# S5 input projections taken out of the preparation and placed around the latents and among the first attention heads

## The chip, the cores and the metric

The kernel runs on one core of one Trainium2 chip. The metric is the device time of one launch in microseconds (us). TensorE (PE) does the matrix products, with its weight loads listed apart as PEld; VectorE (DVE), ScalarE (ACT) and GpSimd (POOL) do elementwise work; SyncE (SP) issues every DMA transfer of this kernel, one after the other from a single queue.

## The reference, cut to what matters

Two layers over 512 tokens of width 1024. The S5 branch takes `u_b`, 1024 of the columns of one combined input projection; the MLA branch takes its latents `c_q` and `c_kv` from the same projection.

```
for l in range(DEPTH):                       # DEPTH = 2
    h = rms_norm(x, pre_norm[l])
    proj = h @ w_in[l]
    z_a, xbc, dt_raw, u_b, z_b, c_q, c_kv, k_rope, z_c, gate_logits = split_columns(proj)
    y_a = ssd_branch(...) @ w_a[l]
    y_b = s5_branch(u_b, z_b, ...) @ w_b[l]  # 64 groups of 16 channels, complex-diagonal scan
    y_c = mla_branch(c_q, c_kv, k_rope, z_c, ...) @ w_c[l]      # 16 heads
    merged = gate_0 * y_a + gate_1 * y_b + gate_2 * y_c
    x = x + rms_norm(merged @ w_o[l], post_norm[l])
```

## The kernel before, in words

Every float32 product is made of three matmuls of a high and a low part. One projection (`proj`, `dense`) takes a tile of 128 output columns: a DMA loads the weights to `wf` (512 KB), ACT rounds them to the high part `wh`, DVE (in the heads every third time POOL) makes the low part `wl`, and PE runs 24 matmuls of 128x512 (lines 116, 117 and 119) on the normed input `hh`, `hl`. `wf`, `wh` and `wl` have two buffers each.

A layer begins with the latents: four projections for `c_q`, two for `c_kv`, each group followed by `normed`. In it PE sums squares (line 225), POOL makes the inverse root `rs_r`, DVE puts it on diagonals (`tmp<-ident,rs_r`), PE spreads it over the partitions (line 231), DVE and ACT scale the latents and split them in `cqh`, `cql`, `ckh`, `ckl`. Then come 16 attention heads. Of head `h+1` the scores are made (`aux<-kh,qh`) before head `h` goes on: DVE masks them and takes the maximum (line 612, then `nm`), ACT makes the exponentials, PE transposes them (line 634), ACT and DVE split them (`ph`, `pl`), PE multiplies with the values (lines 644 to 647). Per pair of heads `make_q` and `make_k` make queries and keys; `ql<-mm,qh` is DVE's share of a query. After each odd head DVE multiplies the pair's output with its gate: `keep<-tmp,keep`, two operands in SBUF.

The S5 preparation `s5_prep` is a generator whose steps run between these parts, whenever `fill(n)` asks for n of them. Its first step makes coefficients on DVE, of which `p_fr` is late and the start of POOL's work. Then follow eight blocks of eight groups. `block` is a step of its own: a projection, a copy `pu` by ACT, a store to the DRAM tensor `ud`, eight transfers back that gather it in another order (`puf`), a store of that to `u2`, three loads of the coefficients `bc`, seven small operations. Then there are four steps `front` (six POOL operations on `pw` and `pv`) with the `back` of the step before: two PE transposes (line 368), splits, matmuls `pM`, every second time a matmul `pk` of full float32 (line 385), and in the fourth a store `msd<-pmo`. There are 42 steps, and the calls of `fill` ask for 42.

After the heads DVE scans the states (`s5_scan`, lines 891 to 894, after a load of `msd`), while PE multiplies with `w_c` and makes gates, with `ah` from the heads' output as its input; the SSD stage, the S5 output and the output projection follow.

The order of each engine's instructions, SP's included, is fixed when the program is made, by a scheduler that goes by the order of the code, by the buffers and by its own idea of durations. On an engine an instruction that waits holds all behind it.

## Time and profile before

| | |
|---|---|
| median of 3 runs | 2001.6 us (2001.11 to 2006.5) |
| the profiled execution | 1999.34 us, of which the span from first to last instruction is 1997.5 us |
| PE, PEld busy | 1883.4 us (94%), 1530.5 us (77%) |
| DVE, ACT, POOL busy | 1448.1 us (72%), 941.1 us (47%), 645.6 us (32%) |
| granted TensorE clock, mean over the span | 0.965 |

A clock of 1 is the higher of TensorE's two levels, 2.4 GHz, and 0.5 the lower, 1.2 GHz; a mean of 0.86 over a stretch says that it stood at the lower level for 28% of it. In a list by time, the number in brackets behind an instruction is the idle time of its engine before it, with what ended that time.

### The profile page before, as it was taken

What the parts mean: (1) busy time and instruction counts of PE and PEld (TensorE: products, weight loads), DVE (VectorE), ACT (ScalarE), POOL (GpSimd) and SP (SyncE); (2) the same over time, 40 slices, a digit from 0 to 9 for tenths busy, and PEclk for the clock granted to TensorE, in tenths of its full rate; (3) what the DMA queues carried; (4) which work ended last, traced back from release to release, by engine and by line L of the source; (5) the groups of instructions that cost most, each with busy time, mean ns of one, the idle gap of its engine ahead of it and who ended that gap; (6) DMA issues with size and microseconds to landing.
All of it is one profiled execution on the core that took longest, in us unless ns stands there. A gap on an engine that the chain in (4) does not pass through costs nothing.

```text
span 1997.5 us, 27806 instructions
## 1 busy us (share of the span) xinstructions
PE 1883.4 (94%) x9688; PEld 1530.5 (77%) x9688; DVE 1448.1 (72%) x2845; ACT 941.1 (47%) x1743; POOL 645.6 (32%) x743
## 2 busy tenths in 40 slices
PE   7897999899999989999998999998999999999998
PEld 5685777687887778888876777776878887788887
DVE  6866667699999857744579666677999996666443
ACT  4364556522555545543333655564235563555431
POOL 1855467301233201201118556672013331012010
PEclk9898999899999999999998999998999999899999
DMA  5333244232312266345223333342232224662541
GB/s 159 94 115 86 88 116 121 74 120 81 131 64 73 70 172 182 106 132 177 96 84 88 112 104 111 91 140 83 96 122 78 75 74 111 182 173 85 166 130 42
DMA packets 132605, 219.96 MB, mean 110 GB/s; under 512 B 36208, under 2 KB 75760, under 8 KB 131952
## 3 DMA queue, kind: packets, MB, share of 16 engines
q1 hardware_dynamic: 132464, 218.19, 36.0%
q8 instruction: 76, 1.25, 0.2%
q14 instruction: 65, 0.53, 0.1%
HBM read 182.08 MB, written 31.33 MB: 107 GB/s over the span
## 4 chain that ended last, share of the span: by engine, by line
PE 59%; DVE 24%; DMA 8%; POOL 3%; ACT 3%; issue 2%; SPq 1%; DVEq 0%; POOLq 0%; ACTq 0%
PE mm L116 13%; PE mm L117 13%; PE mm L119 12%; DVE wl L78 4%; DMA wf<-in_w_in 3%; DVE keep L69 3%; PE mm L61 2%; PE mm L62 2%; PE mm L63 2%; DVE ms L894 2%; DVE sc_t L891 2%; PE pk L385 2%; DVE ms L893 1%; PE aux L61 1%; PE aux L62 1%
## 5 line engine op out<-in xcount | busy, mean ns | idle before, releaser
L116 PE MATMUL mm<-hh,wh 128*128 128x512 f32 (+1 forms) x1232 | 500.9, 407 | 16.0 <-DVE ql L78 8.8
L117 PE MATMUL mm<-hl,wh 128*128 128x512 f32 (+1 forms) x1232 | 493.5, 401 | 0.0
L66 ACT ACTIVATE wh<-wf 128x1024 fp32r<-128x1024 f32 (+1 forms) x294 | 291.4, 994 | 422.9 <-PE mm L117 232.7
L78 DVE TENSOR_TENSOR wl<-wf,wh 128x1024 fp32r<-128x1024 f32 (+1 forms) x243 | 297.0, 1227 | 180.6 <-ACT wh L66 151.9
L119 PE MATMUL mm<-hh,wl 128*128 128x512 f32 (+1 forms) x1232 | 315.4, 393 | 3.8 <-DVE wl L78 3.8
L116 PEld LDWEIGHTS mm<-hh,wh 128*128 128x128 f32 (+1 forms) x1232 | 237.3, 193 | 77.9 <-DVE ql L78 9.9
L117 PEld LDWEIGHTS mm<-hl,wh 128*128 128x128 f32 (+1 forms) x1232 | 236.7, 192 | 50.0 <-issue 1.9
L119 PEld LDWEIGHTS mm<-hh,wl 128*128 128x128 f32 (+1 forms) x1232 | 227.7, 187 | 53.3 <-DVE wl L78 4.6
L81 POOL TENSOR_TENSOR mg<-mg,tmp 128x512 f32<-128x512 f32 x32 | 77.4, 2420 | 461.4 <-DVE tmp L78 244.0
L81 POOL TENSOR_TENSOR wl<-wf,wh 128x1024 fp32r<-128x1024 f32 (+1 forms) x51 | 109.0, 2138 | 291.2 <-PE mm L119 185.9
L116 PE MATMUL mm<-ah,wh 128*128 128x512 f32 x512 | 200.6, 394 | 0.0
L117 PE MATMUL mm<-al,wh 128*128 128x512 f32 x512 | 199.8, 391 | 0.0
L119 PE MATMUL mm<-ah,wl 128*128 128x512 f32 x512 | 127.6, 390 | 0.0
L116 PEld LDWEIGHTS mm<-ah,wh 128*128 128x128 f32 x512 | 96.5, 189 | 21.6 <-issue 1.8
L117 PEld LDWEIGHTS mm<-al,wh 128*128 128x128 f32 x512 | 96.3, 188 | 20.6 <-DVE keep L78 0.5
L119 PEld LDWEIGHTS mm<-ah,wl 128*128 128x128 f32 x512 | 95.7, 188 | 19.5
L612 DVE CUSTOM_DVE_ANT_0 sc<-aux,cmask 128x128 f32<-128x128 f32 (+3 forms) x128 | 60.3, 485 | 50.2 <-PE aux L63 48.4
L81 POOL TENSOR_TENSOR pv<-pq,ar 128x288 f32<-128x288 f32 x64 | 56.7, 906 | 86.3 <-PE pk L385 69.8
L66 ACT ACTIVATE sc<-sc,nm 128x128 f32<-128x128 f32 (+3 forms) x128 | 70.3, 553 | 28.7 <-DVE nm L73 28.7
L78 DVE TENSOR_TENSOR pl<-aux,ph 128x512 fp32r<-128x512 f32 (+1 forms) x96 | 54.7, 593 | 25.6 <-ACT ph L66 25.2
L69 DVE SCALAR_TENSOR_TENSOR keep<-mm,cw,keep 128x511 f32<-128x511 f32 (+2 forms) x96 | 71.0, 740 | 2.1 <-ACT keep L66 1.5
L66 ACT ACTIVATE tmp<-mm 128x512 f32<-128x512 f32 x76 | 44.8, 593 | 58.5 <-PE mm L63 32.3
(344 smaller groups left out, 4083.4 us busy)
## 6 DMA issues: line engine op xcount, KB each, us to landing
wf<-in_w_in SPq DMA_DIRECT2D x156, 512.0 KB
odr<-pv SPq DMA_DIRECT2D x64, 128.0 KB
wf<-in_w_c SPq DMA_DIRECT2D x16, 512.0 KB
wf<-in_w_a SPq DMA_DIRECT2D x16, 512.0 KB
wf<-kpad SPq DMA_DIRECT2D x128, 64.0 KB
wf<-odr SPq DMA_DIRECT2D x16, 512.0 KB
wf<-in_w_glu SPq DMA_DIRECT2D x16, 512.0 KB
wf<-in_w_b SPq DMA_DIRECT2D x16, 512.0 KB
```

What stands on the lines that cost most here:

```text
L61: mm(out, ah, bh, start=start, stop=False)
L62: mm(out, ah, bl, start=False, stop=False)
L63: mm(out, al, bh, start=False, stop=stop)
L66: self.nc.scalar.activation(out, in_, func, **kw)
L69: self.nc.vector.scalar_tensor_tensor(out, in0, s, in1, op0, op1)
L78: self.nc.vector.tensor_tensor(out, a, b, op)
L81: self.nc.gpsimd.tensor_tensor(out, a, b, op)
L116: mm(ps[:m], wh[:, o(i)], bh, start=i == 0, stop=False)
L117: mm(ps[:m], wh[:, o(i)], bl, start=False, stop=False)
L119: mm(ps[:m], wl[:, o(i)], bh, start=False, stop=i == k - 1)
L385: nc.tensor.matmul(pk.rearrange("p g k -> p (g k)"), bbp[b % 2][:, q:q + 4].rearrange("p g h -> p (g h)"), v1[:, :, 0:8].rearrange("p g k ...
L612: nc.vector.tensor_tensor_reduce(out=sc, in0=ps[:, :n], in1=self.cmask[:, 512 - n:512], op0=ALU.add, op1=ALU.max, scale=1.0, scalar=-3.0e3 ...
```

## The change

The projection of a block becomes a method `s5_u` of its own, called by `inputs(n)` from `mla`: two after the latents' projections, one after `normed` of `c_q`, one after `normed` of `c_kv`, and one each in heads 1, 3, 5 and 7. Its copy `pu` is stored by eight transfers (16 partitions, pieces of 64 floats) straight to `u2`, which now has the final order; the tensor `ud` and the gather are gone. In the preparation `load(b)` takes the finished block (`puf`) from `u2` and the `bc` coefficients, one block ahead: it is called in the third step of the block before. `block` is no step any more but opens the first `front`; 34 steps remain, and `fill` asks for 3 steps after every fourth head and for 2 after the others. Half of `bc` gets a second buffer, `pu`, `puf` and `pmo` one buffer each in place of two shared by all three, and a scratch size of the program is lowered.

```diff
--- before.py
+++ after.py
@@ -230,6 +230,16 @@
         pr = self.bank()
         nc.tensor.matmul(pr, self.ones, dg, start=True, stop=True)
         return pr
+
+    def s5_u(self, l, pp, b):
+
+        ps = self.proj(l, UB + b)
+        u = pp.tile([P, 512], F32, name="pu", tag="pu").rearrange("p (j c) -> p j c", j=8)
+        self.act_(u[:, ::-1], ps.rearrange("p (c j) -> p j c", j=8))
+        for g in range(8):
+            self.nc.sync.dma_start(
+                self.u2[b, :, 64 * g:64 * g + 64].rearrange("(j h) c -> h j c", j=8), u[16 * g:16 * g + 16],
+            )
 
 
     def s5_prep(self, l, pp):
@@ -292,40 +302,35 @@
         zero = pp.tile([16, 112], F32, name="zero", tag="pkf")
         nc.vector.memset(zero, 0.0)
         d = lambda nm, shape: self.dr.tile(shape, F32, name=f"{nm}{l}")
-        kpad, odr, msd, u2 = d("kpad", [16, 64, 240]), d("odr", [P, 64, P]), d("msd", [2, 64, 2, 32, 64]), d("u2", [8, P, 512])
-        ud = d("ud", [8, 8, 16, 8, 64])
+        kpad, odr, msd, u2 = d("kpad", [16, 64, 240]), d("odr", [P, 64, P]), d("msd", [2, 64, 2, 32, 64]), self.u2
         nc.sync.dma_start(kpad[:, :, 0:112], zero.unsqueeze(1).broadcast_to([16, 64, 112]))
         self.s5m[l] = (kpad, odr, msd, u2, sc1, sc2)
         yield
         NB = 2
         et = self.gt
-        pf = lambda nm: pp.tile([P, 512], F32, name=nm, tag="pf", bufs=2)
 
         bbp = [pt(f"pbb{i}", [P, 8, 32]) for i in range(2)]
         for t in bbp:
             nc.gpsimd.memset(t, 0.0)
 
-        def block(b):
-
-            ps = self.proj(l, UB + b)
-            u = pf("pu").rearrange("p (j c) -> p j c", j=8)
-            self.act_(u[:, ::-1], ps.rearrange("p (c j) -> p j c", j=8))
-            nc.sync.dma_start(ud[b].rearrange("g h j c -> (g h) j c"), u)
-            uf = pf("puf")
-            for j in range(8):
-                nc.sync.dma_start(
-                    uf[16 * j:16 * j + 16].rearrange("h (g c) -> h g c", g=8),
-                    ud[b, :, :, j].rearrange("g h c -> h g c"),
-                )
-            nc.sync.dma_start(u2[b], uf)
+        def load(b):
+
+            uf = pt("puf", [P, 512])
+            nc.sync.dma_start(uf, u2[b])
             g8 = slice(8 * b, 8 * b + 8)
-            x1, x2 = (pt(n, [P, 8, 2, 16]) for n in ("bc1", "bc2"))
+            x1, x2 = pt("bc1", [P, 8, 2, 16]), pt("bc2", [P, 8, 2, 16], 2)
             nc.sync.dma_start(x1, a["s5_bc"][l, :, g8])
             nc.sync.dma_start(x2[0:64], a["s5_bc"][l, 64:128, g8])
             nc.sync.dma_start(x2[64:128], a["s5_bc"][l, 0:64, g8])
+            return uf, x1, x2
+
+        def block(b, uf, x1, x2):
+
+            g8 = slice(8 * b, 8 * b + 8)
             b1, b2, c1, c2 = x1[:, :, 0], x2[:, :, 0], x1[:, :, 1], x2[:, :, 1]
             fb = lambda x: x[:, g8].unsqueeze(2).broadcast_to([P, 8, 16])
-            u1, bs, q1 = (pt(n, [P, 8, 16]) for n in ("pu1", "pbs", "pq1"))
+            u1 = pp.tile([P, 8, 16], F32, name="pu1", tag="pv2")
+            bs, q1 = (pt(n, [P, 8, 16]) for n in ("pbs", "pq1"))
             bb = bbp[b % 2][:, :, 0:16]
             et(bb, b1, fb(fr), ALU.mult)
             et(u1, b2, fb(fis), ALU.mult)
@@ -360,7 +365,7 @@
             if s == 0:
                 u = keep["u"] = pp.tile([P, 8, 2, 64], F32R, name="pu2", tag="pu2")
                 self.split(uf.rearrange("p (g c) -> p g c", g=8), u[:, :, 0], u[:, :, 1])
-                keep["mo"] = pf("pmo").rearrange("p (g c) -> p g c", g=8)
+                keep["mo"] = pt("pmo", [P, 512]).rearrange("p (g c) -> p g c", g=8)
                 nc.gpsimd.memset(keep["mo"][:, :, 0], 0.0)
             u, mo = keep["u"], keep["mo"]
             pm = self.pq.tile([P, 512], F32, name="pm", tag="pb")
@@ -400,15 +405,16 @@
             if s == 3:
                 nc.sync.dma_start(msd[b // 4, :, :, 8 * (b % 4):8 * (b % 4) + 8].rearrange("p r g c -> r p g c"), mo)
 
-        todo = None
+        todo, nxt = None, load(0)
         for b in range(8):
-            blk = block(b)
-            yield
+            blk = block(b, *nxt)
             for s in range(4):
                 vw = front(b, s, *blk)
                 if todo:
                     back(*todo)
                 todo = (b, s, blk[0], blk[1], *vw)
+                if s == 2 and b < 7:
+                    nxt = load(b + 1)
                 yield
         back(*todo)
 
@@ -473,7 +479,7 @@
         self.gt(mg, mg, g, ALU.add)
 
 
-    def mla(self, l, fill):
+    def mla(self, l, fill, inputs):
         nc, tc, a = self.nc, self.tc, self.a
         with tc.tile_pool(name=f"mla{l}", bufs=1, reuse_waits="tile") as mp:
             qn, kvn = mp.tile([P, 4], F32, name="qn"), mp.tile([P, 2], F32, name="kvn")
@@ -504,9 +510,12 @@
 
             fill(1)
             cq, ckv = latent(CQ, 4), latent(CKV, 2)
+            inputs(2)
             cq = normed(*cq, qn, "cq")
+            inputs(1)
             fill(1)
             ckv = normed(*ckv, kvn, "ck")
+            inputs(1)
 
             def rope(ps, n):
                 sw, r = self.tmp(), self.tmp()
@@ -590,10 +599,12 @@
                     make_k(h // 2 + 1)
                 if h % 4 == 0:
                     make_v(h // 4)
+                if h % 2 == 1 and h < 8:
+                    inputs(1)
                 if h < 15:
                     pr[h + 1] = self.attend_qk(mp, q[h + 1], kt[(h + 1) % 2], h + 1)
                 values(h)
-                fill(3 if h % 2 else 2)
+                fill(3 if h % 4 == 3 else 2)
             self.lo_pool = 0
 
     def attend_qk(self, mp, q, k, h):
@@ -982,13 +993,21 @@
         self.yc = []
         with ExitStack() as pst:
             pp = pst.enter_context(tc.tile_pool(name=f"prep{l}", bufs=1, reuse_waits="tile", side="right"))
+            self.u2 = self.dr.tile([8, P, 512], F32, name=f"u2{l}")
+            todo_u = list(range(8))
+
+            def inputs(n):
+                for b in todo_u[:n]:
+                    self.s5_u(l, pp, b)
+                del todo_u[:n]
+
             prep = self.s5_prep(l, pp)
 
             def fill(n):
                 for _ in range(n):
                     next(prep, None)
 
-            self.mla(l, fill)
+            self.mla(l, fill, inputs)
             fill(99)
         with tc.tile_pool(name=f"act{l}", bufs=8, reuse_waits="tile") as self.act:
             self.mix(l)
@@ -1214,7 +1233,7 @@
     from concourse.bass_utils import run_bass_kernel_spmd
 
     arrays = layouts(inputs)
-    nc = bacc.Bacc("TRN2", target_bir_lowering=False, num_devices=1)
+    nc = bacc.Bacc("TRN2", target_bir_lowering=False, num_devices=1, dynamic_dma_scratch_size=1024)
     aps = {
         n: nc.dram_tensor(f"in_{n}", v.shape, mybir.dt.from_np(v.dtype), kind="ExternalInput").ap()
         for n, v in arrays.items()
```

How the order of the instructions changes is shown at three places of the first layer. The first is POOL, where the latents are normed: `rs_r` is the inverse root that PE waits for, everything else down to the second row of `pbb` belongs to the preparation, except `wl` and `tmp`. Before:

```order
L81 TENSOR_TENSOR pw_1184<-pbb_757,ar 128x256
L81 TENSOR_TENSOR wl<-wf,wh 128x1024
L81 TENSOR_TENSOR pv_1324<-bc_806,ai 128x288
L81 TENSOR_TENSOR pbs<-pbs,pu_810 128x128
L81 TENSOR_TENSOR rs_r<-rs_v,mhalf 128x4
L81 TENSOR_TENSOR tmp<-tmp 128x512
L81 TENSOR_TENSOR pbb_758<-bc_1390,p_fr 128x8x16
```

Now:

```order
L81 TENSOR_TENSOR pv_1493<-bc_886,ai 128x288
L81 TENSOR_TENSOR pv_1331<-pv_1331,pv_1493 128x288
L81 TENSOR_TENSOR pu_1515<-bc_1369,p_fis 128x128
L81 TENSOR_TENSOR pbb_880<-pbb_880,pu_1515 128x8x16
L81 TENSOR_TENSOR rs_r<-rs_v,mhalf 128x4
L81 TENSOR_TENSOR pu_1515<-bc_1368,p_fi 128x128
L81 TENSOR_TENSOR wl<-wf,wh 128x1024
L81 TENSOR_TENSOR rs_r<-rs_v,mhalf 128x4
```

From `p_fr` on, 15 POOL operations (one of them a `wl`) stood ahead of the first `rs_r`; now it is 25, without a `wl`, and the inverse roots of both latents stand close together. In the second layer the count goes from 5 to 20. On PE, 48 projection matmuls (two projections) stood between line 225 and line 231 of `c_q`; now two more projections stand ahead of line 225, 31 matmuls between the two, and 41 behind them, ahead of the first `cqh`.

The second place is SP's queue in the same stretch. `u_388` is the DRAM tensor `u2`, `wf<-in_w_uq` and `wf<-in_w_ukv` are weights that the latents meet next. Now:

```order
L240 DMA u_388<-pu 16x8x64 x8
L102 DMA wf<-in_w_in 128x1024
L361 DMA odr_571<-pv_900 128x2x128
L319 DMA puf<-u_388 128x512
L361 DMA odr_571<-pv_1331 128x2x128
L240 DMA u_388<-pu 16x8x64 x8
L102 DMA wf<-in_w_uq 128x512
L361 DMA odr_571<-pv_1331 128x2x128
L319 DMA puf<-u_388 128x512
L322 DMA bc_1750<-in_s_bc 128x256
L240 DMA u_388<-pu 16x8x64 x8
L102 DMA wf<-in_w_uq 128x512
```

Four groups of eight stores now stand among these weight loads (the fourth, ahead of `wf<-in_w_ukv`, isn't shown), and two loads `puf` that must wait until the stores of the same block have landed. Before, one store `ud` and one group of eight gathers stood there, behind all three of these weight loads.

The third place is PE at the end of the heads, ahead of the first matmul with `w_c` (`mm<-ah,wh`). `pm`, `pM` and `pk` belong to the preparation. Before:

```order
L1009 MATMUL aux<-ident,rs 16x128 x4
L368 MATMUL pm<-ident,pw_4093 128x128 x2
L645 MATMUL aux<-pl,v_3574 64x256
L647 MATMUL aux<-ph,v_3574 128x256
...
L368 MATMUL pm<-ident,pw_4127 128x128 x2
L377 MATMUL pM<-pu_4041,pmh 128x128
L1021 MATMUL aux<-r_4262,sel 128x512 x3
L378 MATMUL pM<-pu_4041,pml 128x64
...
L385 MATMUL pk<-pv_4091,pbb_758 128x512
L1021 MATMUL aux<-r_4262,sel 128x512 x2
L116 MATMUL mm<-ah,wh 128x512
```

Now:

```order
L656 MATMUL aux<-pl,v_3734 64x384
L658 MATMUL aux<-ph,v_3734 128x384
L1028 MATMUL aux<-ident,rs 16x128 x4
L656 MATMUL aux<-pl,v_3734 64x256
L658 MATMUL aux<-ph,v_3734 128x256
L656 MATMUL aux<-pl,v_3734 64x128
L658 MATMUL aux<-ph,v_3734 128x128
L1040 MATMUL aux<-r_4253,sel 128x512 x5
L116 MATMUL mm<-ah,wh 128x512
```

Between the last scores and the first matmul with `w_c` PE had four pairs of `pm`, sixteen `pM` and three `pk` to do; of these one `pk` and four `pM` are left there.

## Rows read from the trace of the kernel before

**Rows 1.** Windows by stage: length, busy time (count) by engine, then clock, DMA share, GB/s.

```profile
core 0: us, PE busy (x) PEld busy (x) DVE busy (x) ACT busy (x) POOL busy (x), PEclk, DMA share, GB/s
62.40:111.70 49.30, 39.65 (x163) 30.21 (x162) 37.19 (x57) 17.40 (x34) 40.09 (x54) 0.86 0.35 100
111.70:368.20 256.50, 235.07 (x1221) 193.52 (x1220) 165.13 (x341) 147.23 (x364) 149.70 (x221) 0.93 0.36 105
368.20:398.40 30.20, 25.00 (x94) 16.90 (x92) 23.35 (x49) 16.43 (x42) 8.57 (x16) 0.72 0.23 56
...
500.00:700.00 200.00, 194.77 (x1062) 157.94 (x1063) 184.67 (x296) 109.47 (x179) 62.58 (x43) 0.99 0.25 84
1055.00:1101.50 46.50, 37.89 (x154) 28.18 (x153) 41.87 (x71) 16.63 (x32) 41.67 (x53) 0.89 0.31 87
1101.50:1353.20 251.70, 235.87 (x1229) 193.52 (x1228) 166.75 (x343) 146.58 (x365) 153.93 (x225) 0.95 0.38 110
1353.20:1385.00 31.80, 26.03 (x95) 17.22 (x93) 23.45 (x49) 16.79 (x42) 8.67 (x16) 0.73 0.23 55
```

**Rows 2.** Timeline of PE in layer 1's latents: start, length, instruction.

```profile
56.99 0.39 PE L116 MATMUL mm<-hh,wh 128*128 128x512 f32 x1
...
62.43 0.95 PE L225 MATMUL aux<-ones,tmp 128*128 128x1 f32 x8
...
77.72 1.12 PE L231 MATMUL aux<-tmp,ones 128*128 128x512 f32 x2 [3.30 <-DVE tmp L73]
...
111.71 0.97 PE L61 MATMUL aux<-kh,qh 96*128 96x128 f32 x3
```

**Rows 3.** Timeline of PE in layer 2's latents.

```profile
1055.02 0.95 PE L225 MATMUL aux<-ones,tmp 128*128 128x1 f32 x8
...
1067.89 1.13 PE L231 MATMUL aux<-tmp,ones 128*128 128x512 f32 x2 [1.56 <-DVE tmp L73]
...
1100.35 0.57 PE L61 MATMUL aux<-kh,qh 96*128 96x128 f32 x3
```

**Rows 4.** Timeline of POOL in layer 1's and layer 2's latents.

```profile
61.88 1.45 POOL L81 TENSOR_TENSOR pbb<-bc,p_fr 128x128 f32<-128x128 f32 x1 [2.19 <-DVE p_fr L78]
...
73.62 1.02 POOL L81 TENSOR_TENSOR rs_r<-rs_v,mhalf 128x4 f32<-128x4 f32 x1
...
1059.40 0.45 POOL L81 TENSOR_TENSOR pbb<-bc,p_fr 128x128 f32<-128x128 f32 x1 [1.78 <-DVE p_fr L78]
```

**Rows 5.** Timeline of SP's queue in layer 1's latents: one group of eight issues.

```profile
77.48 3.82 SPq L316 DMA_DIRECT2D puf<-ud  x8
```

**Rows 6.** The chain that ended last: two stores, start and time to landing.

```profile
175.09 7.77 DMA msd<-pmo
...
1152.76 2.00 DMA ud<-pu
```

**Rows 7.** Timelines of DVE, POOL and PE around the end of head 3.

```profile
150.74 4.87 DVE L78 TENSOR_TENSOR keep<-tmp,keep 128x512 f32<-128x512 f32 x1
...
147.19 1.36 POOL L81 TENSOR_TENSOR pv<-pq,ar 128x288 f32<-128x288 f32 x2 [0.80 <-PE pk L385]
...
155.14 0.97 POOL L81 TENSOR_TENSOR pw<-pbs,ai 128x256 f32<-128x256 f32 x1
...
156.39 0.80 PE L116 MATMUL mm<-hh,wh 128*128 128x512 f32 x1 [4.25 <-DVE ql L78]
```

**Rows 8.** Windows around the same gap, columns as in rows 1.

```profile
152.00:168.00 16.00, 11.75 (x45) 9.16 (x46) 10.67 (x14) 6.05 (x17) 5.37 (x8) 0.79 0.13 42
164.00:172.00 8.00, 8.00 (x40) 6.32 (x39) 6.76 (x10) 3.81 (x9) 5.33 (x7) 1.00 0.34 94
```

**Rows 9.** Timeline of PE in layer 2: the last gap of that kind.

```profile
1360.92 0.39 PE L645 MATMUL aux<-pl,v 128*64 128x384 f32 x1 [2.79 <-DVE pl L78]
```

**Rows 10.** Groups by form, DVE, 111.7 to 368.2: busy us, mean ns | idle before.

```profile
L78 DVE TENSOR_TENSOR keep<-tmp,keep 128x512 f32<-128x512 f32 x7 | 15.7, 2249 | 0.0
L612 DVE CUSTOM_DVE_ANT_0 sc<-aux,cmask 128x512 f32<-128x512 f32 x15 | 10.3, 685 | 1.1 <-PE aux L63 0.5
```

**Rows 11.** Waits over the span: total us, times, longest us.

```profile
POOL pu L81 <- DMA bc<-in_s_bc: 34.3, 13, 6.7
```

**Rows 12.** Timelines of PE and DVE at the end of layer 1's heads.

```profile
367.93 0.39 PE L63 MATMUL aux<-kh,ql 96*128 96x512 f32 x1
...
391.40 0.79 PE L116 MATMUL mm<-ah,wh 128*128 128x512 f32 x1
...
371.98 3.19 DVE L73 TENSOR_SCALAR nm<-mx 128x4 f32<-128x4 f32 x1
...
404.83 0.28 DVE L891 TENSOR_TENSOR sc_t<-sc,ms 128x64 f32<-128x64 f32 x1
```

## The prediction

> **What bounds the kernel now.** The page's first part gives PE 94% of the span, so PE comes first: what PE doesn't use is idle time or clock. I therefore went from the page to windows by stage, and in each stage took its length less PE's busy time, plus the share of it at the missing clock (1 less the mean clock, times the length). For layer 1's latents, 49.30 us long with 39.65 busy at 0.86, that is 9.65 + 6.9 = 16.6 us [rows 1]. In the same way layer 2's latents give 13.7, the heads 39.4 and 28.4, the ends of the heads 13.7 and 14.4. Together 126 us of 1997.5; the change touches all six stretches and cannot win more than that. The rest of the span is almost full, as 500 to 700 us shows: 194.77 of 200 busy at 0.99. DVE has 184.67 there [rows 1], so work moved toward that stretch finds little free.
>
> **The latents.** The work is only moved: one projection is 24 matmuls, 62.43 - 56.99 = 5.44 us of PE, 0.227 us each [rows 2]. What can be won is PE's wait inside this stretch. Line 231 starts at 77.72 after 3.30 us idle [rows 2], although two projections lie between it and line 225. It waits for a chain: POOL's `rs_r`, which starts at 73.62 [rows 4], then DVE's `tmp`, so 77.72 - 73.62 = 4.1 us from `rs_r` to line 231. POOL had begun at 61.88, when `p_fr` came, and did 15 operations in 11.74 us [rows 4]; one was the long `wl`, which I put at 2.4, the others at 0.67.
>
> Now POOL has 25 operations before `rs_r`, without `wl`: 25 x 0.69 = 17.3 us, so `rs_r` starts at 61.9 + 17.3 = 79.2 and line 231 can start at 83.3. PE has two projections more ahead of line 225 (62.43 + 10.9 = 73.3) and 31 matmuls behind it (7.0), and is ready at about 80.4. The wait stays, some 2.9 us. Line 231 and small steps take 2, then come 41 matmuls (9.3), 66 more up to the first scores (24 of a projection, 36 of queries, 6 of keys: 15.0) and 2.5 of small ones: first scores at 83.3 + 2 + 9.3 + 15.0 + 2.5 = 112.1, against 111.71 [rows 2]. By then three more projections (16.3 us) are done, so the best case is a gain of 16.3 - 0.4 = 15.9. The worst is first scores at 125.7: a wait of 2.8 for the first keys, two spells at half clock that lose 3.4 each (the price of one, below), 4 for late weights (SP, below), a gain of 2.3. I take 118.5, in between, since each of these has its counterpart in the trace but not all need come: gain 9.5.
>
> Layer 2 by the same steps: line 225 goes from 1055.02 [rows 3] to 1065.9; 33 matmuls more give 1073.4. POOL starts at 1059.40 [rows 4] and has 20 operations (14.0) instead of 5, so `rs_r` starts at 1073.4, line 231 at 1077.5 after 4.1 idle, where it was 1.56 [rows 3]. First scores: 1105 at best, 1118.6 at worst, I take 1111.5 against 1100.35 [rows 3], 11.2 later with 16.3 done: gain 5 (11.7 to -2). Latents together: **-14.5**.
>
> **SP's queue.** A block has ten transfers and three of `bc` now, and nine and three after: nothing is saved or lost in issues (eight take 3.82 us [rows 5]). What can be late: `puf` is behind its own eight stores and ahead of the weights for queries and keys, and SP goes in order. While `puf` waits for the stores to land, the weights are not issued. The stores write pieces of 256 bytes. Nothing before does exactly that; the nearest rows are `msd`, in pieces of 256 bytes too, 7.77 us to landing, and `ud`, in long rows, 2.00 [rows 6]. With the first, the weights come up to 4 us late at one place per layer (in the worst case above); with the second not at all. The Trainium skill speaks against the new layout: "DMA: Bandwidth & Descriptors", section "Specifications", asks for transfers of at least 512 bytes for the full rate and says that below it the engine reads, modifies and writes. The two landing times agree in direction, though other queueing may be in them. Elsewhere a late `puf` costs nothing, for it is loaded one block ahead.
>
> **The heads.** Three of the seven projections that stood in the heads are in the gain above; the four that remain stand in heads 1 to 7, none in heads 8 to 15. There PE filled with them the time in which it would have waited for masks, exponentials and splits. So some idle time opens: nothing at best, since queries, keys and preparation still fill in; at worst the present idle rate of 256.50 - 235.07 = 21.4 us [rows 1] doubles in half the heads and a bit falls on other work, some 8. I take 3 per layer: **+6**.
>
> **The end of the heads.** From the last scores (367.93) to the first matmul with `w_c` (391.40) PE needs 23.5 us [rows 12], at clock 0.72 [rows 1]: the preparation's last steps and the last head wait for each other. Most of these steps move ahead of it. What is left is the last head's own chain, about 14 us by the same timeline (mask, exponentials, transposes, products). PE's share of the moved steps, some 5 us, is paid earlier. 23.5 - 14 - 5 = 4.5, I take 4 per layer (0 if the chain keeps its length, 9 if the moved work finds free places): **-8**. DVE's `nm`, 3.19 us for 128x4 [rows 12], is in that chain and would be short with POOL quiet.
>
> **The scan.** It begins at 404.83 [rows 12], after the last `msd`, and could begin some 10 us sooner. But what follows it is held by DVE's 184.67 of 200 [rows 1], so at most part arrives: 0 to 8 per layer, I take 2: **-4**. The second `bc` buffer and the smaller scratch I cost at nothing: POOL's waits for `bc`, 34.3 us in 13 times [rows 11], are on an engine 32% busy, and PE asks for its results a step later. What their loss could do is the first rival.
>
> Sum: -14.5 + 6 - 8 - 4 = -20.5, from 1999.3 to 1979; the median lies 2.3 above the profiled execution, so I forecast **1980**. All the good ends together give 2001.6 - 27.6 - 18 - 16 = 1940, all the bad ones 2001.6 - 0.3 + 16 = 2017; they don't come together, so the forecast's own range is 1962 to 1993. What a measurement of this kernel tells from no change is about 0.3%, 6 us.
>
> **Rivals.** *Slower: POOL stands in DVE's way more often.* At the end of head 3, DVE's `keep<-tmp,keep`, two operands in SBUF, takes 4.87 us from 150.74, while POOL goes from one piece to the next from 147.19 to beyond 155.14; it ends only at 155.61. Behind it in DVE's order is `ql`, and PE stands 4.25 us for it at 156.39 [rows 7]. Then the clock falls: 0.79 over 152 to 168, 3.4 us lost, and 1.00 behind it [rows 8]. The seven `keep` of these heads have a mean of 2249 ns where `sc<-aux,cmask` of the same size, one operand not in SBUF, has 685 [rows 10]. I count seven such gaps of PE in both layers, the first [rows 7] and the last, 2.79 us [rows 9], 21.5 us together: 3.1 each and 3.4 of clock, 6.5 us. The Trainium skill names it: "GPSIMD Engine Reference", section "8. Key points", says that the engine shares its SBUF interfaces with VectorE, in contention with DVE instructions that have two SBUF inputs; the 4.87 us agree. Now POOL waits for `bc` no more, a block's small operations run into the first `front`, and nine fronts stand in four heads where there were eight: longer runs without a break. Three more hits eat the gain (3 x 6.5 = 19.5), from the fourth or fifth on it is slower than before; if all 16 ends of odd heads were hit, nine more, 1980 + 58 = 2038. Against it: the work of POOL is the same, it merely has another place, and a hit needs POOL's run and `keep` together. Four to six more, 2006 to 2019, is how it would come: 2012. Chance 0.2.
>
> *Given back.* PE has the same matmuls as before. If heads 8 to 15 open as much idle time as the latents win, the time stays at 2001, give or take 6. For it: PE is 92% busy in the heads. Against: the stretches with most loss per us are the latents and the ends, and both get filled. Chance 0.2.
>
> *SP late.* If the stores land as slowly as `msd` and the weights wait each time, the latents come near their worst ends, 2.3 - 2 = 0.3 where I take 14.5. With two thirds of that lost the time is 1980 + 10 = 1990, at the most 1994: a smaller gain. Chance 0.2.
>
> **Numbers.** Forecast 0.4, SP late 0.2, given back 0.2, slower 0.2. Faster by over 0.3% means below 1995.6: the forecast, nearly all of SP late, and a little of given back: 0.61. Within: most of given back: 0.17. Slower, above 2007.6: the first rival and a tail of the second: 0.22. For 8 in 10 the range goes from 1960 to 2014.
>
> **What would show it.** In the profile after: line 231 at about 83 with 2 to 4 us idle; first scores near 118 and 1111; POOL's wait for `bc` mostly gone; last scores to `w_c` some 14 to 18 us; new idle time in heads 8 to 15 of a few us; the number of PE gaps behind `keep` near seven. Wrong would make me: twelve or more of these gaps, weights for queries landing after PE is ready, or latents that end beyond 125.

## The result, and the profile after

The changed kernel takes 2019.63 us (median of 4 runs, 2016.97 to 2021.86), the kernel before 2001.36 beside it: ratio 1.0085, 95% interval 1.0064 to 1.0106. It is slower by 0.85%, beyond the range that was given. The profiled execution has a span of 2020.0 us, 22.5 more than before. All intervals below are of the ratio to the kernel before, timed on the same chip as the run.

The page of the changed kernel, first part, engines' busy time:

```profile
span 2020.0 us, 27725 instructions
PE 1876.6 (93%) x9688; PEld 1533.8 (76%) x9688; DVE 1429.4 (71%) x2847; ACT 938.8 (46%) x1743; POOL 633.2 (31%) x741
```

PE does the same 9688 matmuls and is busy 6.8 us less than before; the lost time is idle. Windows by stage (columns as in [rows 1]; latents, heads and ends of the heads of both layers, 500 to 700, and then heads 0 to 7 and 8 to 14 of each layer apart):

```profile
72.40:119.30 46.90, 40.55 (x169) 31.50 (x167) 26.59 (x48) 15.64 (x27) 23.72 (x27) 0.93 0.46 114
119.30:378.30 259.00, 228.50 (x1188) 188.18 (x1187) 166.52 (x348) 145.85 (x374) 162.13 (x248) 0.93 0.34 94
378.30:409.70 31.40, 17.89 (x74) 11.91 (x73) 20.67 (x63) 14.54 (x32) 0.31 (x1) 0.78 0.26 79
500.00:700.00 200.00, 193.22 (x1030) 157.21 (x1029) 181.81 (x287) 108.40 (x176) 58.86 (x40) 0.97 0.26 83
1081.90:1124.30 42.40, 39.83 (x170) 31.32 (x169) 29.79 (x50) 16.92 (x31) 28.57 (x33) 0.92 0.49 123
1124.30:1381.70 257.40, 223.99 (x1186) 184.71 (x1185) 172.74 (x347) 144.45 (x370) 160.64 (x246) 0.94 0.34 95
1381.70:1412.20 30.50, 17.25 (x72) 11.64 (x71) 20.78 (x69) 13.48 (x31) 0.31 (x1) 0.78 0.26 81
119.30:263.00 143.70, 130.35 (x664) 107.43 (x663) 84.39 (x185) 79.83 (x202) 87.38 (x129) 0.94 0.35 94
263.00:375.70 112.70, 95.55 (x506) 78.19 (x505) 80.38 (x157) 65.04 (x170) 74.75 (x120) 0.91 0.32 91
1124.30:1262.50 138.20, 125.18 (x661) 103.91 (x660) 88.94 (x184) 79.08 (x198) 85.90 (x127) 0.96 0.36 98
1262.50:1379.00 116.50, 96.11 (x505) 78.14 (x505) 81.83 (x156) 64.15 (x171) 74.69 (x120) 0.91 0.31 89
```

The same halves of the heads before:

```profile
111.70:249.70 138.00, 122.35 (x628) 101.16 (x627) 87.84 (x178) 75.77 (x187) 71.63 (x106) 0.93 0.33 96
249.70:364.70 115.00, 109.22 (x575) 89.55 (x573) 74.36 (x157) 68.96 (x170) 76.19 (x114) 0.94 0.41 120
1100.30:1235.40 135.10, 125.43 (x644) 103.36 (x644) 89.28 (x182) 76.29 (x190) 75.75 (x111) 0.94 0.36 104
1235.40:1349.70 114.30, 108.14 (x574) 88.35 (x573) 75.79 (x157) 68.86 (x170) 77.41 (x114) 0.96 0.41 120
```

"Loss" below is what the prediction used: length less PE's busy time, plus length times missing clock. The latents lose 9.6 and 6.0 us where they lost 16.6 and 13.7 [rows 1]: 14.7 won. The heads lose 48.6 and 48.8, before 39.4 and 28.4: 29.6 more. The ends lose 20.4 and 20.0, before 13.7 and 14.4: 12.3 more. In the heads the loss lies in one half: heads 8 to 14 go from 12.7 and 10.7 to 27.3 and 30.9; heads 0 to 14 together from 66.5 to 98.7, of which PE's idle time makes 37.3 and 63.9 and the clock the rest. Three projections have left heads 8 to 14 (575 matmuls before, 506 now), 16.3 us of work, and its length went from 115.0 to 112.7 and from 114.3 to 116.5. Heads 0 to 7 lose 22.0 and 18.5, before 25.3 and 17.8.

At the end of layer 1's heads, timelines of DVE, PE and SP's queue:

```profile
388.61 0.48 DVE L701 MEMSET dtraw<- 32x512 f32 x1
397.36 0.27 DVE L902 TENSOR_TENSOR sc_t<-sc,ms 128x64 f32<-128x64 f32 x1 [8.27 <-DMA ms<-msd]
397.83 0.68 DVE L69 SCALAR_TENSOR_TENSOR tmp<-aux,tmp 64x512 f32<-64x512 f32 x1
398.85 0.68 DVE L78 TENSOR_TENSOR r<-tmp,r 32x512 fp32r<-32x512 f32 x1
```

```profile
399.68 3.12 PE L1040 MATMUL aux<-r,sel 64*128 64x512 f32 x5 [9.98 <-DVE r L78]
402.73 0.79 PE L116 MATMUL mm<-ah,wh 128*128 128x512 f32 x1
```

```profile
381.25 0.56 SPq L406 DMA_DIRECT2D msd<-pmo  x1
...
389.36 0.32 SPq L898 DMA_DIRECT2D ms<-msd  x1
...
390.21 0.42 SPq L672 DMA_DIRECT2D alog<-in_a_log  x1
```

PE needs `r`. Its operands come by 391.2 (ACT's last copy), but DVE's order has the scan's first `sc_t` ahead of it, and that waits for `ms`, a load that waits on SP for the last `msd` to land (6.8 us, to 389.36). Before, the scan began at 404.83 [rows 12], behind `r`.

### The profile page after: what moved, and what is told of

Read it like the earlier page. It is cut to its first block, busy times and chain, and to the rows that moved or that the text cites. A ratio compares the mean times of both kernels' runs of the same rounds, so it can differ in the third digit from the quotient of the medians.

```text
span 2020.0 us, 27725 instructions
## 1 busy us (share of the span) xinstructions
PE 1876.6 (93%) x9688; PEld 1533.8 (76%) x9688; DVE 1429.4 (71%) x2847; ACT 938.8 (46%) x1743; POOL 633.2 (31%) x741
## 4 chain that ended last, share of the span: by engine, by line
PE 62%; DVE 17%; DMA 12%; ACT 3%; POOL 3%; issue 2%; SPq 1%; DVEq 0%; POOLq 0%; ACTq 0%
PE mm L116 15%; PE mm L117 14%; PE mm L119 14%; DMA wf<-in_w_in 4%; DVE wl L78 3%; DMA msd<-pmo 2%; PE mm L62 2%; PE mm L63 2%; PE mm L61 2%; DVE keep L69 2%; PE aux L61 1%; PE aux L62 1%; PE aux L63 1%; PE pk L390 1%; ACT wh L66 1%
## 5 line engine op out<-in xcount | busy, mean ns | idle before, releaser
L78 DVE TENSOR_TENSOR wl<-wf,wh 128x1024 fp32r<-128x1024 f32 (+2 forms) x245 | 300.0, 1229 | 186.6 <-ACT wh L66 155.1
L116 PEld LDWEIGHTS mm<-ah,wh 128*128 128x128 f32 x512 | 96.2, 188 | 21.9 <-issue 1.2
L117 PEld LDWEIGHTS mm<-al,wh 128*128 128x128 f32 x512 | 96.1, 188 | 20.3 <-issue 0.5
L81 POOL TENSOR_TENSOR pv<-pq,ar 128x288 f32<-128x288 f32 x64 | 51.0, 818 | 54.9 <-PE pk L390 43.0
```

The source lines that it names most:

```text
L78: self.nc.vector.tensor_tensor(out, a, b, op)
L81: self.nc.gpsimd.tensor_tensor(out, a, b, op)
L116: mm(ps[:m], wh[:, o(i)], bh, start=i == 0, stop=False)
L117: mm(ps[:m], wh[:, o(i)], bl, start=False, stop=False)
```

## The experiments

Losses of heads 0 to 7 / 8 to 14 in layer 1 and layer 2, us, worked out from windows of each run in the same way; behind the name the heads with the last four projections (before and in e10 all but one stand in the heads). "Fronts" are those between the first and the last scores of a layer, counted as pairs of `pm` in the trace; the last column is PE's wait for the transfers `qh<-rrh`, both layers together. Losses, fronts and waits are those of one profiled execution (f2's took 2026.1, g2's 2001.6 us), and the clock's two digits alone leave about 0.7 us open in each loss.

| run | median, ratio (95%) | layer 1 | layer 2 | fronts | `qh` |
|---|---|---|---|---|---|
| before (odd heads 1 to 13) | 2001.4 | 25.3 / 12.7 | 17.8 / 10.7 | 24, 25 | 0 |
| changed (1, 3, 5, 7) | 2019.6, 1.0085 (1.0064 to 1.0106) | 22.0 / 27.3 | 18.5 / 30.9 | 30, 30 | 13.1 |
| e2: three dummies in 9, 11, 13 | 2021.5, 1.0114 (1.0094 to 1.0135) | 21.4 / 22.3 | 21.2 / 22.5 | 29, 29 | 8.1 |
| f1: old steps (1, 3, 5, 7) | 1996.9, 0.9981 (0.9963 to 0.9999) | 17.3 / 20.4 | 18.3 / 21.6 | 26, 26 | 10.3 |
| f2: old steps (7, 9, 11, 13) | 2026.8, 1.0110 (1.0064 to 1.0156) | 45.9 / 12.2 | 44.2 / 17.4 | 27, 27 | 17.7 |
| g1: old steps (5, 7, 9, 11) | 1988.5, 0.9947 (0.9932 to 0.9961) | 28.9 / 6.4 | 25.5 / 6.5 | 28, 28 | 13.0 |
| g2: old steps (1, 5, 9, 13) | 2008.0, 1.0033 (1.0014 to 1.0052) | 17.6 / 20.8 | 17.8 / 30.2 | 28, 28 | 12.5 |
| e5: two steps a head (5, 7, 9, 11) | 1991.2, 0.9959 (0.9943 to 0.9974) | 19.8 / 14.4 | 25.2 / 17.6 | 28, 28 | 8.8 |
| g3: two steps a head (3, 6, 9, 12) | 2015.7, 1.0090 (1.0073 to 1.0107) | 17.0 / 26.5 | 20.4 / 33.4 | 28, 29 | 20.3 |
| e10: all in the heads (0, 2, ..., 12) | 2028.4, 1.0138 (1.0118 to 1.0159) | 21.5 / 22.3 | 25.8 / 15.6 | 27, 27 | 15.8 |

**The end of the heads.** e1 makes `sc_t` wait for the last output:

```diff
+        for t in (t1, t2):
+            nc.vector.tensor_copy(t[:, 0, 0:1], self.yc[-1][:, 0:1])
```

> The changed kernel, with the first operations of the scan tied on DVE behind the last multiplication of the heads' outputs (two copies of one column). Theory: the changed kernel lost about 10 us per layer at the end of the heads because DVE's order has sc_t, which waits for the load of ms, ahead of r, for which PE waits at line 1040 (19.4 us in two times). Then both waits vanish and the time falls from 2019.6 by 12 to 19 us, to 2001 to 2008; the heads stay as they are (259 and 257 us). Rival: PE would wait at that place anyway or the scan, begun later, gives it back in the SSD stage: 2015 to 2021.

2020.6, 1.0112 (1.0090 to 1.0133), the rival's time. Last scores to `w_c`: 20.8 and 21.9 us, where 24.4 and 23.3 stood. A second wait took the place of the first (DVE, then PE, of e1):

```profile
393.56 0.17 DVE L75 TENSOR_SCALAR e_zc<-alog 128x16 f32<-128x16 f32 x1 [3.48 <-DMA alog<-in_a_log]
...
393.83 0.68 DVE L78 TENSOR_TENSOR keep<-keep,aux 128x512 f32<-128x512 f32 x1
```

```profile
394.56 0.79 PE L1042 MATMUL aux<-r,sel 64*128 64x512 f32 x1 [4.13 <-DVE keep L78]
```

`alog` is a small load behind `ms` on SP's queue. e7 takes both waits away: e1's edit, and the four small loads into tiles of their own at the start of the layer.

```diff
+        self.small = s("dtb", [P, 16]), s("alog", [P, 16]), s("cw", [P, 16, 4]), s("cb", [P, 16])
+        nc.sync.dma_start(self.small[1], a["a_log"][l:l + 1, :].broadcast_to([P, 16]))
...
```

> The changed kernel with the scan held as in the first run, and with the four small loads (dtb, alog, cw, cb) issued at the start of the layer into tiles of their own. Theory: the load of ms, which waits until the last store of msd has landed, holds SP's queue and then the transfers; behind it wait sc_t and, with the scan held, e_zc, which needs alog; DVE's order puts either ahead of what PE needs for the first matmul with w_c. With both out of the way the stretch from the last scores to w_c falls from 24.4 and 23.3 us to 14 to 17 and the time from 2019.6 to 2001 to 2009. Rival: the end of the heads is bound by its own chain, and 21 us stay as with the scan held alone: 2016 to 2021.

The stretch fell to 16.3 and 16.3 us as foreseen, the time didn't: 2019.45, 1.0094 (1.0079 to 1.0109). Behind the heads the matmuls had become slower, 0.233 us from one to the next (e7), where e13, the same with 64 bytes of padding more, has 0.2275:

```profile
422.12 0.39 PE L116 MATMUL mm<-ah,wh 128*128 128x512 f32 x1
422.35 0.39 PE L117 MATMUL mm<-al,wh 128*128 128x512 f32 x1
422.59 0.39 PE L116 MATMUL mm<-ah,wh 128*128 128x512 f32 x1
422.82 0.39 PE L117 MATMUL mm<-al,wh 128*128 128x512 f32 x1
```

```profile
421.52 0.39 PE L116 MATMUL mm<-ah,wh 128*128 128x512 f32 x1
421.75 0.39 PE L117 MATMUL mm<-al,wh 128*128 128x512 f32 x1
421.98 0.39 PE L116 MATMUL mm<-ah,wh 128*128 128x512 f32 x1
422.20 0.39 PE L117 MATMUL mm<-al,wh 128*128 128x512 f32 x1
```

> The run with the scan held and the small loads first, with 64 bytes of padding more, so that everything allocated behind the small tiles keeps its place within 512 bytes. In the run without it the matmuls with w_c, w_a and w_b took 233 ns in place of 227, and the stretch from the last scores to w_c was 16.3 us, but the time didn't fall. If the place of the tiles took it back, the matmuls are at 227 again and the time is 2016.8 - 10 to 20, 2000 to 2008. Rival (the scan's later start gives it back): 227 ns and 2015 to 2020.

2012.67, 1.0066 (1.0049 to 1.0083), 7 us below the changed kernel, though the two intervals overlap (1.0064 to 1.0106 there), with the stretch again at 16.3 and 16.4 us (windows of e13):

```profile
378.00:394.30 16.30, 10.00 (x53) 6.37 (x51) 12.31 (x27) 11.65 (x29) 0.31 (x1) 0.96 0.37 117
1374.70:1391.10 16.40, 10.08 (x54) 6.40 (x52) 12.41 (x27) 11.75 (x29) 0.31 (x1) 0.95 0.38 118
```

So both waits are shown, 15 us in two layers. In the time at most half of them arrive: the small loads at the start of the layer move line 225 of layer 1 from 72.4 to 77.3, and 5 us come back in the stages from `w_c` on.

**What the projections fill.** e2 adds work that nobody uses:

```diff
+                if h in (9, 11, 13):
+                    self.act_(self.tmp(), self.proj(l, UB))
```

> The changed kernel with three more projections per layer in heads 9, 11 and 13, whose results nobody uses: 72 matmuls or 16.3 us of PE per layer added. Theory: heads 8 to 15 are not bound by PE but by the chain from scores to values, and what left them was filling; then the added work costs at most 5 us per layer, 2019.6 + 0 to 10. Rival: PE is the bound there: 2019.6 + 25 to 33, 2045 to 2053.

32.6 us of PE work more, and the time is 1.8 us above that of the changed kernel (4 us when each is taken against the kernel before beside it). That it fell into the forecast range is in part luck. Heads 8 to 14 grew from 112.7 and 116.5 to 123.0 and 125.0, 10.3 and 8.5 us for 16.3 of work: 6 to 8 us were cover. The rest came back behind: in this order `r` stands ahead of `sc_t`, and from the last scores to `w_c` it takes 18.6 and 18.2 us, together 11 less than in the changed kernel. The loss of both layers' heads is 87.4 us, 11 below the changed kernel's 98.7 (before: 66.5).

f1 gives the steps back their old form, 26 fronts in the heads of each layer where the changed kernel has 30 and the kernel before 24 and 25 (pairs of `pm`):

```diff
             blk = block(b, *nxt)
+            yield
...
-                fill(3 if h % 4 == 3 else 2)
+                fill(3 if h % 2 else 2)
```

> The changed kernel with the preparation's steps as they were: the block a step of its own (42 steps), three and two steps after the heads in turn. Projections, stores and buffers stay as in the change. In the heads there are then 24 to 25 fronts in place of 30. Theory: the heads lose more time (length less PE's work, 71.9 and 69.7 us against 55.3 and 50.0 before) because a quarter more of the preparation runs in them; then this falls to 50 to 58 per layer, and with sc_t behind r again the time is 1985 to 1998. Rival (the projections missing in heads 8 to 15 are the cause): the heads lose 66 to 72 as now, 2010 to 2020. Rival (single buffers of pu, puf and pmo, or the stores): the same 66 to 72.

The time came as forecast. The heads' loss fell by 21 us, from 98.7 to 77.6, most of it in heads 8 to 14; the stretch to `w_c` is 17.8 us in both layers. From `w_c` on the stages take 12 us more than in the changed kernel, which is why the time lies only 4 us below that of before. f2 adds to f1:

```diff
-                if h % 2 == 1 and h < 8:
+                if h in (7, 9, 11, 13):
```

> As the run before it, with the last four projections in heads 7, 9, 11 and 13, where they were before the change. If missing filling is part of the cause, the heads lose 4 to 10 us per layer less than in the run before it; if not, the same within 4. Time: 1978 to 1995 by the theory of the fronts, 2005 to 2020 by the rival of the buffers and stores.

Windows of f2, halves of the heads:

```profile
115.50:263.60 148.10, 121.46 (x589) 98.44 (x587) 88.68 (x183) 76.20 (x197) 90.72 (x137) 0.87 0.27 81
263.60:377.10 113.50, 105.87 (x562) 88.06 (x563) 69.23 (x154) 67.66 (x169) 70.44 (x100) 0.96 0.35 100
1119.40:1266.30 146.90, 121.77 (x587) 98.65 (x585) 88.27 (x183) 75.67 (x193) 89.22 (x135) 0.87 0.29 81
1266.30:1383.80 117.50, 111.84 (x562) 93.41 (x563) 69.71 (x154) 67.44 (x168) 70.02 (x100) 0.90 0.34 96
```

The second half is near that of before (12.2, 17.4); the first, from which three projections went, is 11 us longer than in f1, where they stand in it. In f1 and f2 the loss goes where the projections don't stand. But f2's 2026.8 lies outside both forecasts, and with 27 fronts its heads lose 120 us, the most of the table. Three other places, each by that one line (g1 and g2 with f1's steps; e5 and g3 with `fill(2)` after every head and no step of its own for the block), in the order g1, g2, e5, g3:

> The old steps, the last four projections in heads 5, 7, 9 and 11. Theory: heads 0 to 4 have no projection besides the gates' and lose 5 to 12 us per layer more than with one in 1 and 3; heads 8 to 14 lose 12 to 18 as with two there: 1990 to 2005, not below the run with 1, 5, 9, 13. Rival: as for that run.

> The old steps (as in the run that brought 1996.9), the last four projections spread over heads 1, 5, 9 and 13. Theory: idle time and missing clock gather in the half of the heads that has no projections (in heads 8 to 14, 27.4 and 30.6 us per layer with 1, 3, 5, 7; in heads 0 to 7, 46.1 and 44.2 with 7, 9, 11, 13). With two in each half, heads 0 to 7 lose 18 to 25 and heads 8 to 14 lose 12 to 18 per layer: 1985 to 1998. Rival (it is the order of the single instructions, not the place of the projections): one of the halves over 28 all the same, 2005 to 2025.

> The changed kernel with two preparation steps after every head, so that the last store of msd comes with the last head again, and with the last four projections in heads 5, 7, 9 and 11 in place of 1, 3, 5 and 7. Theory: sc_t stands behind r in DVE's order here, so the 10 us per layer at the end of the heads go, and two projections per layer fill idle time in heads 8 to 15 (some 4 to 8 us per layer), against some 5 us per layer of preparation back in the last head: 1985 to 2003. Rival, that the lost time is due to something that every placement has (the 256-byte stores, POOL's longer runs): 2012 to 2020.

> 34 steps, two after every head, the last four projections in heads 3, 6, 9 and 12 (the version with 5, 7, 9, 11 took 1991.2). Theory: spread more evenly, heads 0 to 7 lose less than the 19.2 and 25.3 us of that version and heads 8 to 14 about its 14.5 and 17.1: 1980 to 1994. Rival (order of single instructions): 2005 to 2025.

e5 came as forecast, g1 better than forecast, g2 and g3 in the rival's range. g1 is the best of all, and it has the least loss in heads 8 to 14 (windows of g1):

```profile
253.90:358.90 105.00, 98.65 (x544) 80.72 (x543) 73.50 (x157) 66.97 (x168) 77.05 (x113) 1.00 0.39 109
1239.50:1345.30 105.80, 99.31 (x545) 80.59 (x544) 74.76 (x157) 66.97 (x168) 76.59 (x113) 1.00 0.39 108
```

But g2 and g3 have two of the four there too and lose 20 to 33. An even spread isn't the answer; my theory of the place alone falls with these two. In g2's layer 2 the longest wait there is one of 8.8 us for `ql`; which instruction stands ahead of which decides beside the number of projections. g1's gain over before isn't in the heads, which lose 67 us in both kernels: its latents lose 15.4 us, before 30.3, while its ends take 24.6 and 24.1 us, no shorter than before.

**The other parts.** e10 (one projection at the latents, the others in heads 0, 2, ..., 12, two steps a head) leaves of the change the stores, the loads and the 34 steps:

> The changed kernel's stores, loads and block, but the projections where they were in the kernel before, or nearly: one at the latents, the others in heads 0, 2, 4, ..., 12, two steps after every head. What is left of the change: stores in 256-byte pieces straight to u2, blocks loaded one ahead, 34 steps. Theory: the latents lose what they won (7 to 9 us per layer beside the version with four there, of 1991), heads 8 to 15 have three projections more and the idle time of before (some 12 us per layer): 1991 to 2005, near the kernel before. Rival (stores in small pieces or the new block cost the time): 2010 to 2025.

2028.4 is above both forecasts. Its latents lose what they lost before or more. Its heads 0 to 14 have the projections of before, and take 263.7 and 266.9 us where before took 253.0 and 249.4; e2, with as many, takes 265.8 in both. So a part of the change that isn't the projections' place makes the heads 11 to 17 us longer per layer, in e10 2.5 and 7.0 of it PE work that no longer stands at the ends. One candidate is the steps (f1); another is in every version with the new stores and loads and in neither the kernel before nor e11 below: PE waits for `qh<-rrh`, 7.3 to 25.1 us in both layers, 15.8 in e10 and 25.1 in e4. No run separates the two. e4 (two at the latents, then 1, 3, 4, 6, 8, 10, the scan held) is the slowest, 2042.74, 1.0213 (1.0192 to 1.0234), 22 us above e1 where its rival said 10 to 20:

> The changed kernel with the scan held as in the first run, and only two projections at the latents, the others in heads 1, 3, 4, 6, 8 and 10. Two projections per layer (10.9 us) go from the latents to the heads, two from heads 5 and 7 to heads 8 and 10 in effect. Theory: the latents lose some 5 us per layer of what they had won, heads 8 to 15 take in two projections at almost no cost: equal to the run with the scan held alone within 8 us, 1995 to 2008. Rival, that the latents' filling is where all the worth lies: 10 to 20 us above that run.

Its latents lose 20 us per layer. f3 gives `pmo` a second buffer; POOL's wait for `msd` behind it, 68.8 us in 13 times in the changed kernel and 7.5 in one before, fell only to 50.8:

> The changed kernel with a second buffer for pmo. POOL's first operation on pmo waits 3.3 us for the store msd of the block before in the trace. If that wait at POOL makes the heads longer, they lose 4 to 8 us per layer less: 2004 to 2012. If not: 2015 to 2022.

2019.35, 1.0085 (1.0062 to 1.0109): nothing, as POOL's waits for `bc`, 34.3 us before and 2.0 now, had bought nothing.

**POOL in DVE's way.** In e8 ACT makes `nm`, in e11 the same in the kernel before, in e12 in e5, in e14 in e5 with e13's small loads. The expectations and the results stand in this order:

```diff
-        self.ts(nm, mx, -SCALE, None, ALU.mult)
+        self.act_(nm, mx, AF.Copy, scale=-SCALE)
```

> The changed kernel with nm (the scaled negative maximum, 128x4) made by ACT in place of DVE, so that POOL's long runs can't hold it on DVE. Rival theory (POOL stands in DVE's way): nm took 12.5 and 17.8 us more than its shortest in the two layers; the waits of PE for pl, mx and ql behind it go, and the heads shorten by 8 to 15 us per layer: 1990 to 2004. Theory (the heads lack filling work in their second half): the heads shorten by 0 to 4 us per layer: 2012 to 2020.

> The kernel before with nm made by ACT in place of DVE, the edit that brought the changed kernel from 2019.6 to 1996.6. If nm behind POOL's runs is what the change made worse (excess on DVE 15.6 us before, 30.3 after), the kernel before gains less, some 4 to 10 us: 1990 to 1996. If the edit helps both alike, 1977 to 1986, it says nothing on the change. Rival (nm isn't the matter, the edit only changed the order at the end of the heads): no gain here, 1998 to 2002.

> Two steps after every head, the last projections in heads 5, 7, 9, 11 (1991.2), with nm made by ACT. Its DVE lost 8.0 and 6.3 us on nm. If these waits reach PE: 1991 minus 6 to 12, 1979 to 1985. If what the projections fill now had hidden them: 1988 to 1993.

> As the run before it, with the four small loads at the start of the layer and the padding; the scan's first operations stand behind r and the first outputs by themselves. Theory: the 4.6 and 4.4 us of waiting for alog at the end of the heads go too and the matmuls keep 227 ns: 6 to 10 us below the run before it, 1971 to 1978. Rival: the later scan or the clock gives it back: as the run before it within 3 us.

1996.56, 0.9985 (0.9974 to 0.9995); 2025.03, 1.0121 (1.0105 to 1.0137); 2024.52, 1.0125 (1.0110 to 1.0140); 2019.99, 1.0095 (1.0071 to 1.0120). One edit gives -23, +25 and +33 us. In e11 the latents and heads of layer 1 end 3 us sooner, but the stages from `w_c` on, where the edit has nothing, go from 663.6 to 674.1 and from 619.6 to 632.3 us: the scheduler has put them in another order. In e12 the 33 us lie in the heads themselves, which go from 244.1 and 251.6 (e5) to 260.6 and 267.1 us from the first to the last scores, though `nm` is off DVE; why isn't known. So these runs don't price the clash. e9b (e5 with e7's small loads) came to 2031.55, 1.0166 (1.0138 to 1.0193), with the slow matmuls of e7, and tells nothing on the wait:

> The version with two steps after every head and the last projections in heads 5, 7, 9, 11, with the four small loads at the start of the layer; the scan isn't held, its first operations stand behind r there already. Theory: in that version DVE's e_zc waits 4.6 us for alog behind the load of ms, and PE 9.0 us in two times for the outputs behind it; this goes: 1991 - 5 to 10, 1981 to 1986. Rival: the wait is covered by something else: 1988 to 1993.

## Why the prediction was wrong

The profiled executions differ by +22.5 us where the sum of the terms was -20.5. Of these 43 us the heads make 24 (+29.6 for +6), the ends of the heads 20 (+12.3 for -8) and the scan 4; the latents came as forecast, and the stages outside these terms give back the other 5. Heads and ends both lie beyond the worst that I had given them, +16 and 0.

- **Latents: right.** 14.7 us won, 14.5 forecast, though by layer 6.9 and 7.7 for 9.5 and 5, so the near agreement is in part luck. In layer 1 line 231 waits as foreseen (83.3 and 2.9 us forecast), and the first scores come at 119.3 (118.5):

```profile
84.18 1.13 PE L231 MATMUL aux<-tmp,ones 128*128 128x512 f32 x2 [3.64 <-DVE tmp L73]
```

- **SP's queue: right for the latents, not for the heads.** PE waits for no weight in the latents, and the rival falls there. But in head 11 of each layer PE now waits 6.5 us for a query's last rows, `qh<-rrh`, which it never did before. SP had stood 7.2 us for POOL's `wl`, then issued two weight loads, the store and these transfers, which took 8.54 us to land. Before, layer 1's were issued at 317.05, and the scores began at 320.91 without a wait. SP's queue after:

```profile
323.84 2.76 SPq L102 DMA_DIRECT2D wf<-in_w_in  x2
326.65 0.59 SPq L406 DMA_DIRECT2D msd<-pmo  x1
327.35 0.60 SPq L554 DMA_DIRECT2D qh<-rrh  x1
```

  PE's wait:

```profile
PE aux L61 <- DMA qh<-rrh: 6.5, 1, 6.5
```

  No run here puts a price on the rule of 512 bytes ("DMA: Bandwidth & Descriptors" of the Trainium skill, "Specifications").
- **Heads: the first step that failed.** I let "some idle time" open, 3 us per layer and 8 at worst; heads 0 to 14 lost 32 us more. I priced the missing projections by PE's present idle time, where PE was 95% busy because of them; with dummies in their place the loss is 11 us smaller (e2). And of the preparation's steps that left the end I had priced only PE's share, 5 us paid earlier, not their operations on POOL, DVE and ACT in the chains of the heads; with the old steps the loss is 21 us smaller (f1). That 11 and 21 make 32 proves no split: each edit gives the whole program another order. With 28 fronts and four projections in the heads the loss is 67 (g1), 77 (e5) or 86 us (g2), with 27 it is 120 (f2). The steps alone are worth 21 us between f1 and the changed kernel and 10 between g1 and e5, which have the same placement. And g1, with fewer projections and more fronts in the heads than before and 13.0 us of wait for `qh<-rrh`, loses about what before loses (67.3 and 66.5 us). So neither count by itself makes the loss, and what in the order makes it stays open. The outcome is the rival "given back", only larger.
- **End of the heads: the second step that failed.** The preparation left it as I said, and a stretch of 16.3 us is there to be had (e7, e13; 14 to 18 forecast). But I took the earlier scan for a gain and overlooked a wait: its first instruction stands ahead of `r` in DVE's order and its load ahead of `alog` in SP's. The stretch went from 23.5 to 24.4 us in layer 1 and from 24.9 to 23.3 in layer 2, with 7.4 and 9.0 us less PE work in it. Forecast -8, measured +12.3, the low clock behind the 10 us wait included.
- **Scan: no gain.** It starts 7.5 us sooner in the trace. From `w_c` to the next line 225 it takes 4.6 us longer than before (two more projections taken off), in the second layer from `w_c` to the end 4.7 us less: together the same.
- **First rival: it moved.** DVE's `keep` is hit less (mean 933 ns in layer 1's heads, 2249 before [rows 10]), DVE's `nm`, one operand, 128x4, more: mean 1030 ns where it was 476. Groups by form of layer 1's heads, after (two rows) and before:

```profile
L73 DVE TENSOR_SCALAR nm<-mx 128x4 f32<-128x4 f32 x15 | 15.4, 1030 | 0.1
L78 DVE TENSOR_TENSOR keep<-tmp,keep 128x512 f32<-128x512 f32 x6 | 5.6, 933 | 0.0
```

```profile
L73 DVE TENSOR_SCALAR nm<-mx 128x4 f32<-128x4 f32 x15 | 7.1, 476 | 0.1
```

  Over the whole span the 32 `nm` take 35.9 us where they took 23.2, the 16 `keep` 15.8 where they took 28.9: together 51.7 and 52.1. Nor does the time on `nm` go with the loss: f2 and g3, whose heads lose 120 and 97 us, have 18.2 and 17.1 us of it, g1 with 67 us has 27.6. So the longer `nm` alone don't explain the heads; how much of them reaches PE stays open. The section of the Trainium skill that the prediction cited ("GPSIMD Engine Reference", "8. Key points") names DVE's 2-port mode beside two SBUF inputs; no run here shows which mode `nm` had.

## What to carry to other kernels

Work that fills waits can be worth most where it stands: before moving it, read how long the stretch would be without it, not how idle the engine is with it. When a move lets a transfer start earlier, look in the new order at what stands behind its first consumer, on that engine and in the queue. And where a scheduler orders the whole program, an edit's time is read stage by stage, since the stages that it doesn't touch moved by 10 us here.

## What the runs showed of the hardware that was not expected

With small tiles of 448 bytes per partition ahead of the others, the 128x512 matmuls with `w_c`, `w_a` and `w_b` took 0.233 us in place of 0.2275 (e7, e9b), for all 1536 some 9 us; with 512 bytes it was gone (e13, e14). Which tile's place makes the difference isn't shown.

DVE's `nm` on 128x4 elements, with a single operand in SBUF, took 4.84 us beside POOL's run, as the two-operand `keep` had [rows 7]; in the kernel before one `nm` took 4.47 us. It ended at 286.04, in the short break of POOL at 286.01 (DVE, then POOL):

```profile
281.20 4.84 DVE L73 TENSOR_SCALAR nm<-mx 128x4 f32<-128x4 f32 x1
```

```profile
285.29 0.72 POOL L81 TENSOR_TENSOR pw<-pw,pw 128x256 f32<-128x256 f32 x1
286.09 0.65 POOL L81 TENSOR_TENSOR pw<-pbs,ai 128x256 f32<-128x256 f32 x1
```
